# Differential attention: the second exponential ahead of the copy of the transposes, a bank for the second transposes, and the values behind all transposes

## The chip, the cores and the metric

The kernel runs on one core of a Trainium2 chip. A time is device microseconds (us) of one execution of the program; lower is better. PE is TensorE, DVE is VectorE, ACT is ScalarE, POOL is GpSimd and SP is the queue that issues most DMAs. PEld is the loading of weights into TensorE, which overlaps the matmuls of PE.

## The reference

One decoder block over 1024 tokens of width 1024: a state-space mixer and differential attention side by side, merged by gates, then a gated feed-forward network. The change lies in the attention. There are 8 heads; each has two softmaxes, whose difference weighs the values:

```python
for i in range(seq // Q_BLOCK):                  # Q_BLOCK = 128: 8 blocks of queries
    q0, q1 = i * Q_BLOCK, (i + 1) * Q_BLOCK
    s = jnp.einsum('bhqd,bhkd->bhqk', q[:, :, q0:q1], k[:, :, :q1]).astype(f32) * scale
    mask = jnp.arange(q1)[None, :] <= jnp.arange(q0, q1)[:, None]
    p = jax.nn.softmax(jnp.where(mask, s, -jnp.inf), axis=-1)
    p = p.reshape(bsz, DA_HEADS, 2, Q_BLOCK, q1)
    attn = (p[:, :, 0] - lam * p[:, :, 1]).astype(v.dtype)
    outs.append(jnp.einsum('bhqk,bhkd->bhqd', attn, v[:, :, :q1]))
...
gate_ssd, gate_att = jnp.split(jax.nn.sigmoid(gates), N_BRANCH, axis=-1)
merged = gate_ssd * (y_ssd @ w_ssd_o[layer]) + gate_att * (y_att @ w_attn_o[layer])
```

## The kernel before

The attention stage goes through 64 items (j, i): 8 heads j, and in each the 8 blocks i of 128 queries. Block i has (i+1)*128 keys. The order on PE, DVE, ACT and POOL is the order in which the code is written; only SP's is left to a scheduler.

- `scores` computes on PE the products of queries and keys of the two softmaxes, s = 0 and s = 1, into tile `sc`, which lies in one of two pairs of PSUM banks (`ps_mm`). For i below 4 both fit into one pair and one call makes them. For i of 4 and more ("long" blocks) each s has a pair of its own. The pairs alternate, so the scores of (t+2, s=1) get the pair of (t+1, s=1) and start when its exponential has read it.
- `maxima` masks and takes the row maxima on DVE (line 1646 for long blocks), `exps` the exponentials with their sums on ACT (1658 for long blocks, 1655 for short ones). `probs` scales and subtracts the two softmaxes on DVE (1666 to 1668); the result is tile `p`.
- `transposes` turns up to four blocks of `p` on PE (1676) into tile `at`, and ACT copies them to `aT` (1677). A long block has eight at most, so two calls, k0 = 0 and k0 = 4; `at` always lies in the one bank `wb`, and the second call's transposes wait for the copy of the first. `values` multiplies `aT` with the values (1687) one item later. In a head's item t the code writes: scores (t+1, s=1), then scores (t+2, s=0), first transposes of t, maxima and exponential of (t+1, s=1), values of t-1, second transposes of t, maxima (t+2, 0), probs (t+1), exponential (t+2, 0).
- Between the scores `fill` puts the second mixer's gate products (`dense_stream`, tile `gap`): 16 halves of 8 steps, three matmuls of 128x512 a step, one or two steps an item. A half ends with a `tanh` on ACT (1578), which frees its bank. The halves rotate over the two banks `wa` together with tile `ot`.
- `out_o` turns four finished blocks (`ot`, 1712), and ACT copies them out (1719; in the last head 1715 and 1716), after `norm_o` has copied the outputs (`osb`, 1694) and POOL has normed them (1695, 1705).
- After the last item a loop of `NLAST` = 20 rounds, n = 0 to 19, does the last 20 gate steps, one a round. Beside them `att_split` splits the attention's outputs, which DMAs bring back from DRAM into `stg`, into high parts on ACT (line 96, tile `oT`) and low parts on DVE. In round 11 the last `out_o` stands ahead of the step. Then follows the attention's output product, tile `ao`.

Of the kernel before, what the change touches and what calls it, by code (L numbers as in the profile page):

```python
# [11 lines left out]
F32 = mybir.dt.float32  # L12
# [5 lines left out]
P = 128  # L18
D = 1024
S = 1024  # L20
HALF = 512
KD = D // P
# [42 lines left out]
def kernel(ctx: ExitStack, tc: tile.TileContext, a: dict, out: bass.AP, dbg=None):  # L65
# [6 lines left out]
    pp = ctx.enter_context(tc.tile_pool(name="pp", bufs=1, space=bass.MemoryType.PSUM))  # L72
# [10 lines left out]
    def ps_mm(name):  # L83
        return pmm.tile([P, 2, HALF], F32, tag="mm", name=name, bufs=2)

    def ps_wa(name):
        return pp.tile([P, HALF], F32, tag="wa", name=name, bufs=2)

    def ps_wb(name):
        return pp.tile([P, HALF], F32, tag="wb", name=name, bufs=1)  # L90
# [177 lines left out]
    with tc.manual_schedule(engines={EN.PE, EN.DVE, EN.Activation, EN.SP}):  # L268
# [96 lines left out]
        for k in range(2, KD):  # L365
            scale_t(k, 0)
            scale_t(k, 1)
            lows = []
# [245 lines left out]
    f = lambda t: t.rearrange("p c h -> p (c h)")  # L614
# [52 lines left out]
    with tc.manual_schedule(engines={EN.PE, EN.DVE, EN.Activation, EN.SP}):  # L667
# [112 lines left out]
        for m, (kind, *_) in enumerate(pairs):  # L780
# [6 lines left out]
            for p in range(7):  # L787
# [64 lines left out]
                if m == 1 and p == 0:  # L852
                    sm1 = SL.get("sm1", F32, (P, 8, 8, NH))
                    sm2 = SL.get("sm2", F32, (P, 1024))
                    dt, la, acum, _, cd, dte, sp0_ = (sm1[:, n] for n in range(1, 8))
# [23 lines left out]
        m = len(pairs) - 1  # L879
# [305 lines left out]
    def fill(n):  # L1185
        for _ in range(n):
            next(stream, None)
# [215 lines left out]
    with tc.manual_schedule(engines={EN.PE, EN.DVE, EN.Activation, EN.SP}):  # L1403
        split_seq(0)
        old = None
        for n in range(4):
            if n == 0:
                fetch_seq(2)
            ps = ps_mm(f"{seq[n][0]}p{seq[n][1]}")
# [53 lines left out]
        for j in range(8):  # L1463
# [7 lines left out]
            ps = so_half(j, 0)  # L1471
# [54 lines left out]
    blocks = list(range(8))  # L1526
# [26 lines left out]
    highs, lows = deque(), deque()  # L1553
# [5 lines left out]
    def dense_stream():  # L1559
        splits[0], raws[1] = seq_w[12], seq_w[13]  # L1560
        for j in blocks:
            fetch(j + 2)
            while highs:
                one(highs)
            while lows:
                one(lows)
            split_later(j + 1)
            w = splits.pop(j)
            for half in range(2):
                ps = ps_wa(f"gap{j}_{half}")  # L1570
                for k in range(KD):
                    xh_, xl_ = hT[k][half][:, 0, :], hT[k][half][:, 1, :]
                    T.matmul(ps, w[0][:, k, :], xh_, start=(k == 0), stop=False)
                    T.matmul(ps, w[0][:, k, :], xl_, start=False, stop=False)
                    T.matmul(ps, w[1][:, k, :], xh_, start=False, stop=(k == KD - 1))
                    if k < KD - 1:
                        yield
                A.activation(gev[:, half, :], ps, AF.Tanh, scale=0.5)
                SP.dma_start(gad[j][:, half * HALF : (half + 1) * HALF], gev[:, half, :])
                yield  # L1580
# [8 lines left out]
            SP.dma_start(vt[b][:, kt, :], vd[kt][:, j * P : (j + 1) * P])  # L1589

    stream = dense_stream()

    def fill(n):
        for _ in range(n):
            next(stream, None)

    items = [(j, i) for j in range(8) for i in range(8)]

# [49 lines left out]
    def exps(t, s):  # L1648
        if t >= len(items):
            return  # L1650
        i = items[t][1]
        L, bq, sc = (i + 1) * P, i % 2, sc_of.pop((t, s))
        if i < 4:
            for s in range(2):
                A.activation(pt_(t, s)[:, :L], sc[:, s, :L], AF.Exp, bias=nmx[bq][0][:, s : s + 1], accum_out=ssum[bq][:, s : s + 1])
            return
        p = pt_(t, s)[:, :L]
        A.activation(p.rearrange("p (h t) -> p h t", h=2) if i == 4 else p, sc, AF.Exp, scale=-1.0, bias=nmx[bq][s][:, 0:1], accum_out=ssum[bq][:, s : s + 1])  # L1658
# [11 lines left out]
    def transposes(t, k0):  # L1670
        j, i = items[t]
        nk = min(4, i + 1 - k0)
        ptr = ps_wb(f"at{j}_{i}_{k0}")
        at = aTs[t % 2][:, k0 // 4]
        for k in range(nk):
            T.transpose(ptr[:, k * P : (k + 1) * P], pt_(t, 0)[:, (k0 + k) * P : (k0 + k + 1) * P], ident)  # L1676
        A.copy(at[:, :nk].rearrange("p k q -> p (k q)"), ptr[:, : nk * P])  # L1677
# [29 lines left out]
        return [first, second]  # L1707

    def out_o(j, grp):
        ptr = ps_wa(f"ot{j}_{grp}")  # L1710
        for qi in range(4):
            T.transpose(ptr[:, qi * P : (qi + 1) * P], ob[:, qi, :], ident)
        if j == KD - 1:
            o = oT[j][grp] = new_hl(f"oT{j}_{grp}")
            A.activation(oe, ptr, AF.Copy, scale=subw)
            A.activation(o[:, 0, :], oe, AF.Copy)
            V.tensor_tensor(o[:, 1, :], oe, o[:, 0, :].bitcast(F32), op=ALU.subtract)
            return
        A.activation(oe, ptr, AF.Copy, scale=subw)
        SP.dma_start(atd[j][:, grp * HALF : (grp + 1) * HALF], oe)  # L1720
# [3 lines left out]
    parts = [(k, half) for half in range(2) for k in range(KD - 1)]  # L1724
    n_att, n_in = 0, 0
# [31 lines left out]
    NFIRST, NLAST = 6, 20  # L1757
# [4 lines left out]
    with tc.manual_schedule(engines={EN.PE, EN.DVE, EN.Activation, EN.Pool}):  # L1762
# [10 lines left out]
        for t, (j, i) in enumerate(items):  # L1773
            quota = (j * sum(share) + sum(share[: i + 1])) * nfill // (8 * sum(share)) - done
            done += quota
            f1 = (quota + 1) // 2
            if long_(t + 1):
                scores(t + 1, 1)
            fill(f1)
            scores(t + 2, 0)  # L1780
            fill(quota - f1)
            transposes(t, 0)
            if long_(t + 1):
                maxima(t + 1, 1)
                exps(t + 1, 1)
            if t > 0:
                values(t - 1)
            if i >= 4:
                transposes(t, 4)
            maxima(t + 2, 0)  # L1790
            if i % 4 in (1, 2) and norm:
                norm.pop(0)()
            else:
                one(lows)
            probs(t + 1)
            exps(t + 2, 0)
            if i % 4 == 3 and pend is not None:
                out_o(*pend)
                pend = None
            if i % 4 == 0 and t > 0:  # L1800
                jj, ii = items[t - 1]
                pend = jj, ii // 4
                norm = norm_o(*pend)
            else:
                one(highs)
            if t == 56:
                SL.put(*qst[0], *kst[0], *klo[0], vt[0])
                stg = [SL.get(f"stg{i}", F32, (P, 2, HALF)) for i in range(2)]
                for _ in range(4):
                    att_in()  # L1810
            if j < 7 and i == 1:
                load_heads(j + 1)
# [5 lines left out]
        for n in range(NLAST):  # L1818
            if n == 4:
                SP.dma_start(srow2, crowd.broadcast_to([P, D]))  # L1820
            elif n > 4 and n % 2 == 0 and n < 16:
                ada_load()
            if 14 < n < 18:
                ada_sum(False, True)
            if n in (4, 7):
                norm.pop(0)()
            if n == 11:
                out_o(*pend)
            if n == 1:
                fetch_ao(0)  # L1830
            fill(1)
            if n < len(parts):
                att_split()
            if n == 13:
                split_ao(0)
        assert n_att == len(parts) and not highs and not lows
        SL.put(osb, gev, mstrip, *stg)
        for k in range(KD):
            SL.put(*hT[k])
# [39 lines left out]
        for j in range(KD):  # L1879
            w = w_ao.pop(j)  # L1880
            ps = ps_mm(f"ao{j}")
# [768 lines left out]
```

## Time and profile before

| | |
|---|---|
| median of three runs | 1825.58 us (1823.63 to 1826.5) |
| the profiled execution | 1825.24 us |
| its span, first to last instruction | 1823.5 us |
| PE busy in the span | 1770.0 us (97%) |
| DVE busy | 1345.5 us (74%) |
| ACT busy | 916.5 us (50%) |
| the attention's items, by the timeline | about 699.8 to 983.4 us of the span |
| the 20 rounds after them | 983.4 to 1004.8 us |

The profile's times are microseconds from the start of the span. A row of the timeline gives the start, the duration, the engine, the line, the operation, its tiles, and in square brackets how long the engine had stood idle before it and what it waited for. A row of the waits gives who waited for whom, the sum, how often, and the longest. The row of a PE matmul has a modelled end, 0.39 us after its start for 128x512, though the next one starts 0.23 us after it; the idle time of PE is therefore shorter in the profile than the delay of the next matmul, and that of PEld is nearer to it.

### The profile page before, as it was taken

Reading aid. Unit: us, or ns where it says so; the run is one execution under the profiler, and the core shown is the slowest. Engines: PE = TensorE matmul, PEld = TensorE weight load, DVE = VectorE, ACT = ScalarE, POOL = GpSimd, SP = SyncE. Lnnn points to the kernel's source line nnn. Section 1 sums busy time; section 2 is a strip of 40 time slices with the busy share of each in tenths; the row PEclk is TensorE's granted clock in tenths of the full one; section 3 lists DMA queues with packets and bytes.
Section 4 is the critical chain, followed back from the end, with each engine's and each line's share of the span. In section 5 each row is a group of like instructions: output and inputs, shape, how many; then the busy total and the mean of one; then the engine's idle time right before and its main releaser. Section 6 shows DMA issues by size and latency. Waiting matters only on the chain.

```text
span 1823.5 us, 23829 instructions
## 1 busy us (share of the span) xinstructions
PE 1770.0 (97%) x8563; PEld 1459.8 (80%) x8563; DVE 1345.5 (74%) x2048; ACT 916.5 (50%) x1642; POOL 175.8 (10%) x183
## 2 busy tenths in 40 slices
PE   7999999999999999999998999999999999999998
PEld 5788888888778887777776888888888888888887
DVE  7887568854767787777776876678998888876545
ACT  7554345456765213556655132655454454564532
POOL 0000000002551200121111003100000000000001
PEclk9999999999999999999999999999999999999999
DMA  9465653375667798654644979313332223378754
GB/s 375 185 202 169 179 144 99 116 255 166 226 208 236 172 377 231 193 154 129 174 132 141 334 250 378 138 64 110 104 130 107 88 100 118 112 237 305 249 155 157
DMA packets 148330, 337.29 MB, mean 185 GB/s; under 512 B 15570, under 2 KB 50290, under 8 KB 148212
## 3 DMA queue, kind: packets, MB, share of 16 engines
q1 hardware_dynamic: 145012, 325.28, 54.6%
q0 software_dynamic: 3200, 10.49, 1.5%
q8 instruction: 67, 1.10, 0.3%
q14 instruction: 51, 0.42, 0.1%
HBM read 240.46 MB, written 95.25 MB: 184 GB/s over the span
## 4 chain that ended last, share of the span: by engine, by line
PE 56%; DVE 6%; ACT 4%; DMA 3%; issue 2%; SPq 1%; POOL 1%; DVEq 0%; ACTq 0%; POOLq 0%
PE upx L2015 4%; PE upx L2014 4%; PE upx L2016 4%; PE upy L2015 2%; PE upy L2014 2%; PE upy L2016 2%; PE o L1687 2%; PE sc L1612 2%; PE dx L2410 2%; PE dx L2411 2%; PE dx L2409 2%; PE dy L2410 2%; PE dy L2409 2%; PE dy L2411 2%; PE mix L2088 2%
## 5 line engine op out<-in xcount | busy, mean ns | idle before, releaser
L2014 PE MATMUL upx<-t,wu_t 128*128 128x512 f32 x264 | 103.2, 391 | 0.5 <-DVE cv L2474 0.4
L2015 PE MATMUL upx<-t,wu_t 128*128 128x512 f32 x264 | 102.9, 390 | 0.2 <-DVE t L2145 0.2
L2016 PE MATMUL upx<-t,wu_t 128*128 128x512 f32 x264 | 102.8, 389 | 0.0
L1988 ACT ACTIVATE wu_t<-sab 128x512 fp32r<-128x512 f32 x57 | 34.1, 627 | 127.9 <-DVE sab L2005 127.9
L1677 ACT COPY aT<-at 128x512 f32<-128x512 f32 (+2 forms) x96 | 46.0, 479 | 96.4 <-PE at L1676 96.4
L97 DVE TENSOR_TENSOR g_lo<-gst,g_hi 128x1024 fp32r<-128x1024 f32 (+1 forms) x42 | 47.5, 1134 | 50.7 <-ACT g_hi L96 50.6
L1612 PE MATMUL sc<-kst,qst 128*128 128x512 f32 (+3 forms) x192 | 67.2, 355 | 11.4 <-ACT p L1658 11.4
L96 ACT ACTIVATE g_hi<-gst 128x1024 fp32r<-128x1024 f32 (+1 forms) x42 | 41.6, 989 | 67.0 <-DMA gst<-gld_s 36.6
L1687 PE MATMUL o<-vt,aT 128*128 128x128 f32 x576 | 74.8, 275 | 0.0
L1687 PEld LDWEIGHTS o<-vt,aT 128*128 128x128 f32 x576 | 69.3, 192 | 0.6
L1646 DVE CUSTOM_DVE_ANT_0 sc<-sc,mstrip 128x640 f32<-128x640 f32 (+3 forms) x64 | 65.4, 1032 | 5.5 <-PE sc L1613 5.5
L2533 POOL TENSOR_TENSOR rsf<-rsf,nhalf 128x1 f32<-128x1 f32 x8 | 5.2, 655 | 624.3 <-DVE rsf L2532 624.3
L1613 PE MATMUL sc<-klo,qst 128*128 128x512 f32 (+3 forms) x192 | 63.7, 341 | 0.0
L1676 PE MATMUL at<-ident,p 128*128 128x128 f32 x288 | 48.1, 276 | 14.5 <-DVE p L1668 14.4
L1658 ACT ACTIVATE p<-sc,nmx 128x640 f32<-128x640 f32 (+3 forms) x64 | 61.6, 964 | 0.0
L541 PE MATMUL xx<-xt,xw_t 128*128 128x512 f32 x156 | 61.0, 391 | 0.5 <-DVE xcv L830 0.5
L2032 DVE SCALAR_TENSOR_TENSOR ug<-cg,vec,ug 128x1023 f32<-128x1023 f32 (+1 forms) x44 | 56.3, 1279 | 6.1 <-ACT ug L2031 5.3
L543 PE MATMUL xx<-xt,xw_t 128*128 128x512 f32 x156 | 60.7, 389 | 0.0
L542 PE MATMUL xx<-xt,xw_t 128*128 128x512 f32 x156 | 60.7, 389 | 0.0
L2014 PEld LDWEIGHTS upx<-t,wu_t 128*128 128x128 f32 x264 | 49.6, 188 | 11.7 <-DVE cv L2474 1.3
L1992 DVE TENSOR_TENSOR wu_t<-sab,wu_t 128x512 fp32r<-128x512 f32 x57 | 39.3, 689 | 26.5 <-ACT wu_t L1988 26.5
L2015 PEld LDWEIGHTS upx<-t,wu_t 128*128 128x128 f32 x264 | 49.6, 188 | 10.6 <-DVE t L2145 0.5
(579 smaller groups left out, 5725.1 us busy)
## 6 DMA issues: line engine op xcount, KB each, us to landing
adas<-in_w_ada SPq DMA_DIRECT2D x32, 512.0 KB
wuf<-in_w_up SPq DMA_DIRECT2D x22, 512.0 KB
gld_s<-gsum SPq DMA_DIRECT2D x22, 512.0 KB
gst<-gld_s SPq DMA_DIRECT2D x20, 512.0 KB
wdt_raw<-wtd SPq DMA_DIRECT2D x20, 512.0 KB
wuv<-in_w_up SPq DMA_DIRECT2D x19, 512.0 KB
gld_a<-ug SPq DMA_DIRECT2D x33, 256.0 KB
adat<-in_w_ada SPq DMA_DIRECT2D x16, 512.0 KB
```

Source lines behind the costliest of these rows:

```text
L541: T.matmul(o, wh, xh_, start=(k == 0 and first), stop=False, skip_group_check=not first)
L1612: T.matmul(sc, qs_[s][:, tsl], ks_[s][:, n0:n1], start=True, stop=False)
L1613: T.matmul(sc, qs_[s][:, tsl], kl[s][:, n0:n1], start=False, stop=True)
L1646: V.tensor_tensor_reduce(out=sc, in0=sc, in1=strip, scale=-1.0, scalar=BIG, op0=ALU.add, op1=ALU.min, accum_out=nmx[bq][s][:, 0:1])
L1658: A.activation(p.rearrange("p (h t) -> p h t", h=2) if i == 4 else p, sc, AF.Exp, scale=-1.0, bias=nmx[bq][s][:, 0:1], accum_out=ssum[bq][ ...
L1687: T.matmul(po_of[j, grp][:, qi, :], aTs[t % 2][:, kt // 4, kt % 4, :], vt[j % 2][:, kt, :], start=(kt == 0), stop=(kt == i))
L2014: T.matmul(out_, wh, xh_, start=(k == 0 and first), stop=False, skip_group_check=not first)
L2015: T.matmul(out_, wh, xl_, start=False, stop=False, skip_group_check=not first)
L2016: T.matmul(out_, wl, xh_, start=False, stop=(k == end), skip_group_check=not first)
L2409: T.matmul(o, gh[:, kk, tsl], wh, start=(k == 0 and not more), stop=False, skip_group_check=more)
L2410: T.matmul(o, gh[:, kk, tsl], wl, start=False, stop=False, skip_group_check=more)
L2411: T.matmul(o, gl[:, kk, tsl], wh, start=False, stop=(k == KF - 1), skip_group_check=more)
```

## The change

Four edits, all in the attention stage. In an item the maxima and the exponential of (t+1, s=1) are written ahead of the first transposes; the second transposes follow the first, and the values come after both; the second transposes, and `ot`, get bank `wa1`, and all gate halves bank `wa0`, one after the other, where they rotated over the two. A `fill` that would step over the end of a half stops there and owes the rest to the next call. The last `out_o` moves from round 11 to round 14.

```diff
-    def ps_wa(name):
-        return pp.tile([P, HALF], F32, tag="wa", name=name, bufs=2)
+    n_wa = 0
+
+    def ps_wa(name, i=None):
+        nonlocal n_wa
+        if i is None:
+            i, n_wa = n_wa % 2, n_wa + 1
+        return pp.tile([P, HALF], F32, tag=f"wa{i}", name=name, bufs=1)
...
-                ps = ps_wa(f"gap{j}_{half}")
+                ps = ps_wa(f"gap{j}_{half}", 0)
...
     def fill(n):
-        for _ in range(n):
+        nonlocal owed, n_step
+        n, owed = n + owed, 0
+        for m in range(n):
+            if m and n_step % KD == 0:
+                owed = n - m
+                return
             next(stream, None)
+            n_step += 1
...
-        ptr = ps_wb(f"at{j}_{i}_{k0}")
+        ptr = ps_wa(f"at{j}_{i}_{k0}", 1) if k0 else ps_wb(f"at{j}_{i}_{k0}")
...
-        ptr = ps_wa(f"ot{j}_{grp}")
+        ptr = ps_wa(f"ot{j}_{grp}", 1)
...
             fill(quota - f1)
-            transposes(t, 0)
             if long_(t + 1):
                 maxima(t + 1, 1)
                 exps(t + 1, 1)
+            transposes(t, 0)
+            if i >= 4:
+                transposes(t, 4)
             if t > 0:
                 values(t - 1)
-            if i >= 4:
-                transposes(t, 4)
             maxima(t + 2, 0)
...
-            if n == 11:
+            if n == 14:
                 out_o(*pend)
...
             fill(1)
+            if n == NLAST - 1:
+                fill(0)
```

What the engines then get is shown at two places, with the names numbered: `sc4_5_1` is head 4, block 5, s = 1, and `at4_4_0` head 4, block 4, k0 = 0; `p1` holds s = 1. The line numbers of the changed kernel are some ten higher.

ACT in head 4, from the first transposes of block 4 on, before and then changed:

```order
L1677 COPY aT0_5702<-at4_4_0_7171 128x512
L1658 ACTIVATE p1_1_5701,ssum1_5710<-sc4_5_1_7150,nmx1_1_5714 128x768
L1677 COPY aT0_5702<-at4_4_4_7183 128x128
L1658 ACTIVATE p0_2_5699,ssum0_5709<-sc4_6_0_7163,nmx0_0_5711 128x896
L1694 COPY osb_5704<-o4_0_7052 128x512
L1677 COPY aT1_5703<-at4_5_0_7206 128x512
L1658 ACTIVATE p1_0_5700,ssum0_5709<-sc4_6_1_7193,nmx0_1_5712 128x896
L1677 COPY aT1_5703<-at4_5_4_7220 128x256
```

```order
L1670 ACTIVATE p1_1_5701,ssum1_5710<-sc4_5_1_7150,nmx1_1_5714 128x768
L1689 COPY aT0_5702<-at4_4_0_7173 128x512
L1689 COPY aT0_5702<-at4_4_4_7179 128x128
L1670 ACTIVATE p0_2_5699,ssum0_5709<-sc4_6_0_7163,nmx0_0_5711 128x896
L1706 COPY osb_5704<-o4_0_7052 128x512
L1670 ACTIVATE p1_0_5700,ssum0_5709<-sc4_6_1_7193,nmx0_1_5712 128x896
L1689 COPY aT1_5703<-at4_5_0_7208 128x512
L1689 COPY aT1_5703<-at4_5_4_7214 128x256
```

The exponential of s = 1 now stands ahead of both copies; nothing else on ACT moves there.

PE at the same place, before and then changed:

```order
L1575 MATMUL gap4_0_7159<-hT1_0_80,ga4_lo_6775 128x512
L1676 MATMUL at4_4_0_7171<-ident_72,p0_0_5697 128x128 x4
L1687 MATMUL o4_0_7052<-vt0_5689,aT1_5703 128x128 x4
L1676 MATMUL at4_4_4_7183<-ident_72,p0_0_5697 128x128
L1612 MATMUL sc4_6_1_7193<-kst0_1_5510,qst0_1_5508 128x512
L1613 MATMUL sc4_6_1_7193<-klo0_1_5584,qst0_1_5508 128x512
```

```order
L1580 MATMUL gap4_0_7159<-hT1_0_80,ga4_lo_6775 128x512
L1688 MATMUL at4_4_0_7173<-ident_72,p0_0_5697 128x128 x4
L1688 MATMUL at4_4_4_7179<-ident_72,p0_0_5697 128x128
L1699 MATMUL o4_0_7052<-vt0_5689,aT1_5703 128x128 x4
L1624 MATMUL sc4_6_1_7193<-kst0_1_5510,qst0_1_5508 128x512
L1625 MATMUL sc4_6_1_7193<-klo0_1_5584,qst0_1_5508 128x512
```

The values have moved behind the second transposes; what follows is the same.

PE in the rounds after the items, around the end of the half `gap7_0` (round 11), before and then changed; `b12` is a part of the gates' input:

```order
L1575 MATMUL gap7_0_8281<-hT6_0_263,ga7_lo_7954 128x512
L1712 MATMUL ot7_1_8335<-ident_72,osb_5704 128x128 x4
L1573 MATMUL gap7_0_8281<-hT7_0_265,ga7_hi_7953 128x512
L1574 MATMUL gap7_0_8281<-hT7_0_265,ga7_hi_7953 128x512
L1575 MATMUL gap7_0_8281<-hT7_0_265,ga7_lo_7954 128x512
L1573 MATMUL gap7_1_8353<-b12_0_3168,ga7_hi_7953 128x512
```

```order
L1580 MATMUL gap7_0_8281<-hT7_0_265,ga7_lo_7954 128x512
L1578 MATMUL gap7_1_8344<-b12_0_3168,ga7_hi_7953 128x512
L1579 MATMUL gap7_1_8344<-b12_0_3168,ga7_hi_7953 128x512
L1580 MATMUL gap7_1_8344<-b12_0_3168,ga7_lo_7954 128x512
L1578 MATMUL gap7_1_8344<-b12_1_3170,ga7_hi_7953 128x512
L1579 MATMUL gap7_1_8344<-b12_1_3170,ga7_hi_7953 128x512
L1580 MATMUL gap7_1_8344<-b12_1_3170,ga7_lo_7954 128x512
L1724 MATMUL ot7_1_8362<-ident_72,osb_5704 128x128 x4
```

The transposes `ot7_1` now come two steps after the end of the half, and `gap7_1` is in the bank of `gap7_0`.

ACT there, before and then changed:

```order
L96 ACTIVATE oT3_1_8332<-stg1_7980 128x512
L1715 ACTIVATE osb_5704<-ot7_1_8335,subw_3458 128x512
L1716 ACTIVATE oT7_1_8340<-osb_5704 128x512
L1578 ACTIVATE gev_5705<-gap7_0_8281 128x512
L96 ACTIVATE oT4_1_8349<-stg1_7980 128x512
```

```order
L101 ACTIVATE oT3_1_8332<-stg1_7980 128x512
L1583 ACTIVATE gev_5705<-gap7_0_8281 128x512
L101 ACTIVATE oT4_1_8340<-stg1_7980 128x512
L101 ACTIVATE oT5_1_8348<-stg0_7979 128x512
L101 ACTIVATE oT6_1_8354<-stg0_7979 128x512
L101 ACTIVATE wao0_hi_8357<-wao0_raw_8250 128x1024
L1727 ACTIVATE osb_5704<-ot7_1_8362,subw_3458 128x512
L1728 ACTIVATE oT7_1_8367<-osb_5704 128x512
```

The tanh of `gap7_0` stands behind the same eleven splits (rounds 0 to 10) in both; the last copies out of PSUM have moved behind the remaining splits and behind the first split of the output product's weights, `wao0`.

More of the change, by code (lines that the diff above doesn't have):

```diff
@@ L1591 @@
     stream = dense_stream()
+    owed = n_step = 0
     def fill(n):
-        for _ in range(n):
+        nonlocal owed, n_step
[4 more added lines that the diff above has]
+                return
             next(stream, None)
+            n_step += 1
     items = [(j, i) for j in range(8) for i in range(8)]
@@ L1835 @@
                 split_ao(0)
-        assert n_att == len(parts) and not highs and not lows
+        assert n_att == len(parts) and not highs and not lows and n_step == 2 * KD * len(blocks)
         SL.put(osb, gev, mstrip, *stg)
```

## The prediction

> **What bounds the kernel now.** I read the page first, then the stage by windows, then the stage's waits, then the timeline of one head.
>
> ```profile
> span 1823.5 us, 23829 instructions
> PE 1770.0 (97%) x8563; PEld 1459.8 (80%) x8563; DVE 1345.5 (74%) x2048; ACT 916.5 (50%) x1642; POOL 175.8 (10%) x183
> ...
> 699.80:983.40 283.60, 256.90 (x1634) 222.91 (x1634) 210.44 (x478) 169.68 (x410) 46.32 (x45) 1.00 0.54 154
> 856.90:873.55 16.65, 14.71 (x91) 12.71 (x92) 13.45 (x30) 11.37 (x26) 3.09 (x3) 1.00 0.52 144
> ```
>
> The two lower rows are windows: bounds, length, then PE, PEld, DVE, ACT and POOL busy. PE is the bound, and in the attention's items it still stands idle 26.7 of 283.6 us; that is the most any reordering can take. The second row is the long-block half of head 4, where PE idles 1.9 us and DVE is busy 13.45 of 16.65. What PE waits for, from the stage's waits (us in total, times, longest):
>
> ```profile
> PEld sc L1612 <- ACT p L1658: 16.6, 24, 1.0
> PE at L1676 <- DVE p L1668: 14.4, 16, 1.3
> PE sc L1612 <- ACT p L1658: 11.4, 24, 0.8
> PEld gap L1573 <- ACT osb L1719: 1.4, 2, 0.7
> ...
> PE upx L2014 <- DVE cv L2474: 0.4, 1, 0.4
> ```
>
> 24 times, three a head, scores wait for an exponential to free their banks; 16 times, two a head, transposes wait for DVE's result `p`. For the scores, PE's own row counts 11.4 us, the weight loads' 16.6; since a matmul normally starts before the modelled end of the one ahead of it, the larger is the delay, and the smaller its lower bound. The last row is the longest wait of PE behind the attention: what is won there is not waited away later.
>
> **The score waits.** Head 4, from its timeline (start, duration):
>
> ```profile
> 854.99 0.60 ACT L1578 ACTIVATE gev<-gap 128x512 f32<-128x512 f32 x1 [1.80 <-PE gap L1575]
> 856.90 0.19 PEld L1612 LDWEIGHTS sc<-kst,qst 128*128 128x128 f32 x1 [0.65 <-ACT p L1658]
> 859.01 0.14 DVE L1646 DVE_READ_ACCUMULATOR2_ANT nmx<- 128x1 f32 x1
> 860.61 0.59 ACT L1677 COPY aT<-at 128x512 f32<-128x512 f32 x1 [2.30 <-PE at L1676]
> 861.09 0.91 ACT L1658 ACTIVATE p<-sc,nmx 128x768 f32<-128x768 f32 x1
> 861.89 0.20 ACT L1658 ACTIVATION_READ_ACCUMULATOR p<-sc,nmx 128x1 f32 x1
> 862.14 0.19 PEld L1612 LDWEIGHTS sc<-kst,qst 128*128 128x128 f32 x1 [0.75 <-ACT p L1658]
> 864.52 0.14 DVE L1646 DVE_READ_ACCUMULATOR2_ANT nmx<- 128x1 f32 x1
> 865.85 1.01 ACT L1658 ACTIVATE p<-sc,nmx 128x896 f32<-128x896 f32 x1
> 867.01 0.19 PEld L1612 LDWEIGHTS sc<-kst,qst 128*128 128x128 f32 x1 [0.63 <-ACT p L1658]
> ```
>
> The middle wait is the plainest. The maxima of block 5 were ready at 859.15, yet the exponential began at 861.09: ACT stood 2.30 us in front of the copy, which waited for PE's transposes. With the exponential ahead it starts about 1.9 us earlier, and 0.75 suffices. For block 6 the maxima were ready at 864.66 and the exponential began at 865.85: 1.2 earlier, 0.63 suffices. For block 4 the gap is alike (0.65); in this head a tanh (854.99) also stands ahead of it, which leaves a tenth or two. So all 24 waits go, but for that. The copies come later instead, by an exponential at most, and nobody needs them before the values of the next item, some 4 us on.
>
> Not all of it reaches the end of the head, because DVE is next:
>
> ```profile
> 839.38 0.63 PE L1676 MATMUL at<-ident,p 128*128 128x128 f32 x4 [0.97 <-DVE p L1668]
> ...
> 864.45 0.39 PE L1613 MATMUL sc<-klo,qst 128*128 128x512 f32 x1
> 864.99 1.23 DVE L1646 CUSTOM_DVE_ANT_0 sc<-sc,mstrip 128x1024 f32<-128x1024 f32 x1 [0.33 <-PE sc L1613]
> 867.68 1.15 DVE L1668 SCALAR_TENSOR_TENSOR p<-p,coef,p 128x896 f32<-128x896 f32 x1
> 869.13 0.62 PE L1676 MATMUL at<-ident,p 128*128 128x128 f32 x4
> 869.89 0.14 DVE L1646 DVE_READ_ACCUMULATOR2_ANT nmx<- 128x1 f32 x1
> 870.32 1.12 ACT L1658 ACTIVATE p<-sc,nmx 128x1024 f32<-128x1024 f32 x1
> 872.12 1.28 DVE L1668 SCALAR_TENSOR_TENSOR p<-p,coef,p 128x1024 f32<-128x1024 f32 x1
> 873.55 0.63 PE L1676 MATMUL at<-ident,p 128*128 128x128 f32 x4 [0.98 <-DVE p L1668]
> ```
>
> From the last score of block 7, s = 0 (864.45), DVE works without a break through maxima, norm and `probs` to the `p` of block 6 at 868.83; PE's transposes start 0.15 behind such a `p` (873.55 against 872.12 + 1.28), so 4.53 after 864.45. PE comes to them after 4.68, of which 0.63 is the third score wait; without it after 4.05. It then waits some 0.5 there: a new wait. For block 7 the maxima are ready at 870.03 and the exponential began at 870.32, so its `p`, and the wait behind it (873.55), come only some 0.2 earlier. Of the third wait 0.2 comes through. Per head 0.65 + 0.75 + 0.2 = 1.60 of 2.03, so in all 16.6 x 1.60 / 2.03 = **-13.1 us**; by the lower row, 11.4, it is -9.0, and with the third wait in full -16.6.
>
> **The bank for the second transposes, and all transposes ahead of the values.** Before, the values covered the copy that the second transposes waited for. With a bank of their own they need no cover; the copies' ACT time is the same. `ot` shares their bank, behind the values of block 6 (14 matmuls), which cover a copy of 0.59. Cost nothing; without that bank the second transposes would wait for exponential and copy.
>
> **One bank for the gates.** A half's first step now waits for the tanh of the half before. At the start:
>
> ```profile
> 707.97 0.39 PE L1573 MATMUL gap<-b,w_gate_hi 128*128 128x512 f32 x1
> 709.61 0.59 ACT L1578 ACTIVATE gev<-gap 128x512 f32<-128x512 f32 x1
> 712.04 0.52 PE L1676 MATMUL at<-ident,p 128*128 128x128 f32 x3 [0.57 <-DVE p L1668]
> ...
> ACT gev L1578 <- PE gap L1575: 6.9, 9, 1.8
> ```
>
> The second half would start at 710.25 (709.61 + 0.59 and a hand-over of 0.05, as at 862.14) instead of 707.97: 2.3, of which the wait of 0.57 at 712.04 absorbs its part: **+1.7**. At the other boundaries among the items ACT mostly stands ready (the last row: 9 of 16 tanhs found ACT waiting for the gate product), and the next step can start 0.39 + 0.60 + 0.1 = 1.1 after the last matmul's start; four score matmuls between take 0.45 to 0.92 and the step's own 0.23, so a wait is at most 0.4. Four or five boundaries have so little between: **+0.9**. The two waits for `osb` in the list above (1.4) belong to the shared rotation and go: **-1.4**. A `fill` that stops early moves single steps by half an item; on SP some loads of the next head's keys stand one place later, behind a store of `osb`, and they are written six items ahead of their use. Neither costs anything.
>
> **The rounds after the items.**
>
> ```profile
> 986.16 0.60 ACT L1578 ACTIVATE gev<-gap 128x512 f32<-128x512 f32 x1 [0.56 <-PE gap L1575]
> 993.95 1.05 PE L1712 MATMUL ot<-ident,osb 128*128 128x128 f32 x4 [3.06 <-POOL osb L1705]
> 995.21 1.94 ACT L96 ACTIVATE oT<-stg 128x512 fp32r<-128x512 f32 x3 [1.52 <-DMA stg<-atd]
> 997.06 0.67 ACT L1715 ACTIVATE osb<-ot,subw 128x512 f32<-128x512 f32 x1
> 997.78 0.79 PE L1573 MATMUL gap<-b,ga_hi 128*128 128x512 f32 x1 [1.51 <-ACT osb L1715]
> 994.00:996.30 2.30, 2.27 (x7) 1.45 (x7) 0.87 (x2) 1.07 (x2) 0.00 (x0) 0.51 0.86 240
> 997.80:1000.60 2.80, 2.80 (x7) 2.22 (x8) 1.23 (x3) 1.71 (x3) 0.00 (x0) 0.50 0.95 288
> 1000.60:1004.80 4.20, 4.20 (x20) 3.44 (x19) 2.61 (x4) 2.21 (x3) 0.00 (x0) 0.97 0.85 308
> ```
>
> (The last three are windows; the third number from the end is the granted clock.) Round 12 waited for ACT's copy at 997.06, which stood behind splits that wait for DMAs. Now the tanh of round 11 stands in that slot (0.60 for 0.67), and round 12 needs it: PE restarts at 997.7, as before. But it has done less: the transposes have moved behind round 13, and cost 0.5 there. In front of the restart PE runs out of work: round 4 begins at 986.81 behind the tanh, the 24 matmuls of eight steps at some 0.23 end at 992.3, and it idles 5.4 us in one piece instead of 3.06 and 1.51. Before, the clock was half from 994.0 to about 1000.6, and 2.8 us of that lay behind the restart. Now it is half behind the restart for 2.8 us to 6.6; that loses 1.4 to 3.3 us where 1.4 were lost. Middle: 0.5 + 0.9 = **+1.4** (0.5 to 2.4).
>
> [...]
>
> **The sum.** -13.1 + 1.7 + 0.9 - 1.4 + 1.4 = -10.5 us. The profiled execution took 1825.24 us; 1825.24 - 10.5 = **1814.7 us**. The median shown, 1825.58, is 0.34 above that execution, within the spread of the three.
>
> **Rivals.** First: DVE takes over one block earlier, so that the second score wait, too, turns into a wait for `p`. Then 0.65 + 0.2 of 2.03 come through, 7.0 us; with the other terms -4.4, 1820.8 us. For it: DVE is busy 81% in the long blocks. Against it: the exponential that starts 1.9 us earlier lets the `p` of block 5 start earlier as well. Chance 0.11.
>
> Second, the other side: the gates pay at every half's end what they pay at the start. Thirteen halves end among the items; the gain without them is 13.1 + 1.4 - 1.4 = 13.1, so at 1.0 us each nothing is left, from 1.3 the kernel is measurably slower, and at 2.3 it takes 1842 us (1825.24 - 13.1 + 29.9). It decides if ACT reaches the tanh late: exponentials and splits of weights stand ahead of it, as at 709.61. Against it stand the nine tanhs for which ACT was waiting. [...] Chance 0.04.
>
> Third: the exponential gains nothing, since something else than the copy holds it, and the score waits stay. Then 1.7 + 0.9 - 1.4 + 1.4 = +2.6, 1827.8 us, hardly to be told from no change: a measurement of this kernel tells about 0.2% (3.7 us). Against it, the maxima were ready 1.2 to 1.9 us early. Chance 0.05.
>
> **How the numbers follow.** The forecast has 0.78, a third wait won in full (1808 to 1810) 0.02. The forecast's own bounds: best -16.6 + 0.9 - 1.4 + 0.5, start absorbed, 1808.6; worst -9.0 + 2.3 + 2.5 + 2.4, 1823.4. As these do not all fall together, and the first rival belongs in it, the range is 1809 to 1820.8. Faster: 0.78 + 0.02 + most of 0.11 = 0.89; same 0.07; slower 0.04.
>
> **What the profile after would show.** Right: the rows `sc <- ACT p` gone or below 2 us; three waits a head for `p`, the new one of 0.3 to 0.5 at block 6; the starts of block 7's transposes some 1.6 us closer from head to head (873.55 - 839.38 = 34.2 for head 4, so 32.6); a wait of `gap` for the tanh of about 2.3 at the start; PE idle over 5 us near the end of the rounds. Wrong: score waits that stay; a wait for `p` at block 5; many waits of `gap` for `gev`; second transposes that wait for a copy; a half clock for longer than 7 us after the rounds' gap.

## The result and the profile after

| | before | after |
|---|---|---|
| median | 1826.04 us (1823.63 to 1826.79, four runs) | 1814.88 us (1812.19 to 1814.98, four runs) |
| ratio, 95% interval | | 0.9938 (0.992 to 0.9955) |
| profiled execution / span | 1825.24 / 1823.5 us | 1814.90 / 1813.1 us |
| first gate step (start of the items) | 699.84 | 697.92 |
| items, to the end of the last values | 283.51 | 273.16 |
| rounds, to the first matmul of `ao` | 21.43 | 22.27 |
| behind the rounds, to the end of the span | 818.72 | 819.75 |

The kernel is 0.6% faster, against a forecast of 1814.7 us. Of the 10.4 us between the two spans, items and rounds make 10.35 - 0.84 = 9.5. The remaining 0.9 is the difference of two places without an edit: the part ahead of the items was 1.9 us shorter, the part behind the rounds 1.0 longer. In the traces of this study the first gate step stands anywhere from 697.92 to 700.96, so that part of the close hit is luck. Below, I therefore compare items and rounds, not spans.

The page's head after:

```profile
span 1813.1 us, 23867 instructions
...
PE 1766.1 (97%) x8563; PEld 1459.4 (80%) x8563; DVE 1347.0 (74%) x2048; ACT 918.0 (51%) x1642; POOL 175.9 (10%) x183
```

The items as one window (length, then PE, PEld, DVE, ACT and POOL busy; the granted clock is third from the end):

```profile
697.90:971.10 273.20, 253.35 (x1634) 223.14 (x1633) 211.42 (x478) 171.02 (x410) 46.33 (x45) 0.99 0.56 159
```

PE's idle time in the items fell from 26.7 to 19.9 us (273.20 - 253.35). That is less than the 10.35 us won: PE's busy time fell as well, by 3.55, since it covered a part of each score wait (modelled ends, and 0.50 for the first matmul behind a wait where the next has 0.39, as at 856.90 and 857.24 before). The mean clock is 0.99 now; it was 1.00.

The waits in the items after:

```profile
ACT p L1670 <- DVE nmx L1658: 34.2, 26, 2.6
PE at L1688 <- DVE p L1680: 14.2, 20, 1.3
...
PEld gap L1578 <- ACT gev L1583: 4.2, 7, 2.6
PE at L1688 <- ACT ga_hi L1553: 3.3, 3, 1.1
PEld at L1688 <- PE sc L1625: 3.2, 7, 0.5
...
PEld sc L1624 <- ACT p L1670: 0.2, 1, 0.2
```

The 24 score waits (16.6 us) have become one of 0.2. ACT now waits for DVE's maxima (first row), where it stood in front of a copy before. PE's waits for `p` are 20 and 3: a row put down to `ga_hi` is the same wait under another name, as block 7 in the next fence shows (1.11 us, 0.15 behind DVE's `p`). That is three a head, the third at block 6 (seven times also as a PEld row that names `sc`).

Head 4 after, from the timeline:

```profile
845.42 0.52 PE L1688 MATMUL at<-ident,p 128*128 128x128 f32 x3 [0.85 <-DVE p L1680]
852.86 0.91 ACT L1670 ACTIVATE p<-sc,nmx 128x768 f32<-128x768 f32 x1 [0.45 <-DVE nmx L1658]
854.20 0.75 ACT L1689 COPY aT<-at 128x512 f32<-128x512 f32 x2 [0.35 <-PE at L1688]
861.68 0.95 PE L1688 MATMUL at<-ident,p 128*128 128x128 f32 x7 [0.35 <-DVE p L1680]
864.82 1.28 DVE L1680 SCALAR_TENSOR_TENSOR p<-p,coef,p 128x1024 f32<-128x1024 f32 x1
866.25 1.06 PE L1688 MATMUL at<-ident,p 128*128 128x128 f32 x8 [1.11 <-ACT ga_hi L1553]
```

The exponential of block 5 (852.86) starts when its maxima are ready; the copies (854.20, both in one row) come behind it. The new wait is 0.35 us at block 6; block 2 (0.85) and block 7 (1.11) wait as before.

How much a head costs is read from the values of block 7, the only groups of 16: first and last of the eight, after and then before:

```profile
738.36 1.95 PE L1699 MATMUL o<-vt,aT 128*128 128x128 f32 x16
969.13 1.95 PE L1699 MATMUL o<-vt,aT 128*128 128x128 f32 x16
```

```profile
739.28 1.95 PE L1687 MATMUL o<-vt,aT 128*128 128x128 f32 x16
981.40 1.95 PE L1687 MATMUL o<-vt,aT 128*128 128x128 f32 x16
```

From the first to the last, seven heads took 230.77 us for 242.12: 32.97 a head for 34.59, so 1.62 less. Head 0 (from the first gate step to the start of its values of block 7) took 40.44 for 39.44, so 1.0 more. Why, and what the rounds did, the timeline shows (two rows of the start, two of the rounds):

```profile
707.69 0.59 ACT L1583 ACTIVATE gev<-gap 128x512 f32<-128x512 f32 x1
708.34 0.50 PE L1578 MATMUL gap<-b,w_gate_hi 128*128 128x512 f32 x1 [2.12 <-ACT gev L1583]
984.75 0.58 ACT L1583 ACTIVATE gev<-gap 128x512 f32<-128x512 f32 x1
985.38 0.80 PE L1578 MATMUL gap<-b,ga_hi 128*128 128x512 f32 x1 [5.12 <-ACT gev L1583]
```

And a window behind each wait:

```profile
709.50:712.90 3.40, 3.40 (x13) 2.92 (x12) 1.13 (x2) 2.24 (x6) 0.00 (x0) 0.52 1.02 245
985.40:989.40 4.00, 4.00 (x12) 3.25 (x13) 0.86 (x2) 1.17 (x2) 0.00 (x0) 0.50 0.85 289
```

At the start PE stands 2.12 us for the tanh, and from 1.3 us after it restarts, the granted clock is half for 3.4 us; nothing like that was forecast. In the rounds PE stands 5.12 us, and the clock is half for 4.1 us behind it (until 989.5).

### The profile page after: what moved, and what is told of

Read it like the earlier page. It is cut to its first block, busy times and chain, and to the rows that moved or that the text cites. A ratio compares the mean times of both kernels' runs of the same rounds, so it can differ in the third digit from the quotient of the medians.

```text
span 1813.1 us, 23867 instructions
## 1 busy us (share of the span) xinstructions
PE 1766.1 (97%) x8563; PEld 1459.4 (80%) x8563; DVE 1347.0 (74%) x2048; ACT 918.0 (51%) x1642; POOL 175.9 (10%) x183
## 4 chain that ended last, share of the span: by engine, by line
PE 48%; DVE 11%; DMA 6%; ACT 4%; issue 3%; POOL 1%; SPq 0%; DVEq 0%; POOLq 0%; ACTq 0%
PE upx L2029 4%; PE upx L2028 4%; PE upx L2030 4%; PE o L1699 2%; DMA gst<-gld_s 2%; PE upy L2029 2%; PE upy L2028 2%; PE upy L2030 2%; PE mix L2102 2%; PE mix L2104 2%; PE mix L2103 2%; PE so L123 2%; PE so L125 2%; PE so L124 2%; PE sc L1625 1%
## 5 line engine op out<-in xcount | busy, mean ns | idle before, releaser
L1658 DVE CUSTOM_DVE_ANT_0 sc<-sc,mstrip 128x640 f32<-128x640 f32 (+3 forms) x64 | 65.5, 1032 | 13.5 <-PE sc L1625 13.1
L1688 PE MATMUL at<-ident,p 128*128 128x128 f32 x288 | 42.5, 274 | 17.5 <-DVE p L1680 14.2
L2029 PEld LDWEIGHTS upx<-t,wu_t 128*128 128x128 f32 x264 | 49.6, 188 | 10.5 <-DVE t L2159 0.5
```

The costliest lines, as they stand in the source:

```text
L1658: V.tensor_tensor_reduce(out=sc, in0=sc, in1=strip, scale=-1.0, scalar=BIG, op0=ALU.add, op1=ALU.min, accum_out=nmx[bq][s][:, 0:1])
L2029: T.matmul(out_, wh, xl_, start=False, stop=False, skip_group_check=not first)
```

## The experiments

Theory A: the order on ACT (the exponential ahead of the copies) is the whole gain; the bank and the values' place only keep the second transposes from waiting, and the single gate bank costs something at the start and in the rounds. Theory B, in several forms: bank and order carry a part of it. Each kernel ran four or five times (`values between` eleven times) beside the kernel before. "Head 0", "a head" (the mean of heads 1 to 7) and "rounds" are from each kernel's one trace, in us. How far one trace can be trusted shows where kernels are alike: a head takes 32.97, 32.96 and 32.97 us in three of them (after, rounds in two banks, second bank at the start), but the rounds, alike in seven of them, take 21.41 to 23.71.

| kernel | median | ratio, 95% interval | head 0 | a head | rounds |
|---|---|---|---|---|---|
| before | 1825.3 to 1826.0 | 1 | 39.44 | 34.59 | 21.43 |
| after | 1814.88 | 0.9938 (0.992 to 0.9955) | 40.44 | 32.97 | 22.27 |
| exponential alone | 1814.30 | 0.9934 (0.9922 to 0.9946) | 37.61 | 33.20 | 22.09 |
| all but the exponential | 1833.36 | 1.0039 (1.0026 to 1.0051) | 43.26 | 35.23 | 22.17 |
| without the bank | 1842.95 | 1.0086 (1.0071 to 1.01) | 43.56 | 36.96 | 22.23 |
| values between | 1823.54 | 0.9988 (0.9979 to 0.9997) | 41.58 | 34.10 | 22.37 |
| seven steps first | 1814.22 | 0.9937 (0.9924 to 0.9949) | 38.67 | 33.06 | 23.31 |
| second bank at the start | 1813.67 | 0.9936 (0.9923 to 0.995) | 38.39 | 32.97 | 21.41 |
| rounds in two banks | 1810.22 | 0.9916 (0.9902 to 0.9929) | 38.86 | 32.96 | 15.61 |
| `probs` ahead of the norm | 1812.12 | 0.9924 (0.9911 to 0.9936) | 40.22 | 32.57 | 23.71 |
| seven steps, rounds, `probs` | 1807.80 | 0.9897 (0.9882 to 0.9913) | 38.19 | 32.79 | 15.20 |
| exponential alone, rounds | 1811.38 | 0.9922 (0.9909 to 0.9934) | 37.63 | 33.21 | 14.94 |
| second bank, rounds, `probs` | 1806.32 | 0.9894 (0.988 to 0.9907) | 37.88 | 32.60 | 14.94 |

**The exponential alone.** The kernel before, with one move:

```diff
-            transposes(t, 0)
             if long_(t + 1):
                 maxima(t + 1, 1)
                 exps(t + 1, 1)
+            transposes(t, 0)
```

> The kernel before, with only the maxima and the exponential of (t+1, s=1) written ahead of the first transposes; banks, values between the transposes and the last round stay as before. Theory A (the gain is the order on ACT alone): the 24 score waits for the exponential are gone, the first gate half still has a second bank, no 2.1 us wait at the start and no 5 us gap in the rounds; against that the second transposes, which share a bank with the first, now wait for a copy that stands behind an exponential, covered by the values: up to 1 us in the last blocks of a head. Together 1814 to 1818 us, ratio 0.993 to 0.996. Theory B (the exponential needs the second bank and the new order to be worth anything): second transposes wait as long as the scores waited, 1824 to 1828 us.

1814.30 us: not to be told from the whole change. Theory A, though not all score waits go: 5.0 us of them stay, at 16 places. Its waits in the items:

```profile
PEld at L1676 <- ACT aT L1677: 9.4, 9, 1.1
...
PE at L1676 <- DVE p L1668: 7.1, 9, 0.8
...
PEld sc L1612 <- ACT p L1658: 5.0, 16, 0.4
```

Block 6 of head 6, from the timeline (the exponential of block 7 and the copy on ACT, the second transposes on PE):

```profile
929.02 1.11 ACT L1658 ACTIVATE p<-sc,nmx 128x1024 f32<-128x1024 f32 x1 [2.00 <-DVE nmx L1646]
930.13 0.58 ACT L1677 COPY aT<-at 128x512 f32<-128x512 f32 x1
930.76 0.55 PE L1676 MATMUL at<-ident,p 128*128 128x128 f32 x3 [0.91 <-ACT aT L1677]
```

With one bank for both, the second transposes wait for the copy only where it stands behind an exponential that itself waits for the maxima, once a head, in block 6 (0.9 us on PE's row). Elsewhere the values between cover the copy. Against these 9.4 us and the 5.0 of score waits, the waits for `p` are shorter by 10.4: 9 of 7.1 us in all, where the whole change has 23 of 17.5. A head is 0.23 longer than with the whole change, 1.6 over seven heads, and head 0 is 2.8 shorter. So bank, order and gates together bring 1.6 us and cost 2.8 at the start.

**All but the exponential.** The changed kernel with maxima and exponential of (t+1, s=1) behind both transposes.

> The changed kernel with the exponential of (t+1, s=1) put back behind the transposes; the banks, all transposes ahead of the values and the last transposes in round 14 stay changed. Theory A: the score waits are back (about 16 us by the weight loads), the costs of the single gate bank stay, so 1826 to 1830 us, ratio 1.000 to 1.0025. Theory B (bank and order carry the gain): 1814 to 1818 us.

1833.36 us, above Theory A's band too. The sign is A's; the size was missed by at least 3 us. Its score waits in the items:

```profile
PEld sc L1624 <- ACT p L1670: 22.3, 31, 1.0
```

Head 4, from the timeline (ACT twice, PEld twice):

```profile
865.52 0.75 ACT L1689 COPY aT<-at 128x512 f32<-128x512 f32 x2 [2.29 <-PE at L1688]
866.16 0.92 ACT L1670 ACTIVATE p<-sc,nmx 128x768 f32<-128x768 f32 x1
867.22 0.19 PEld L1624 LDWEIGHTS sc<-kst,qst 128*128 128x128 f32 x1 [0.98 <-ACT p L1670]
877.32 0.19 PEld L1624 LDWEIGHTS sc<-kst,qst 128*128 128x128 f32 x1 [0.29 <-ACT p L1670]
```

With both transposes ahead, the exponential stands behind two copies instead of one. The wait of 0.75 became 0.98, and a fourth (0.29) came ahead of block 7's transposes: 22.3 us instead of 16.6. That makes a head 0.64 longer than before, 4.5 us over seven heads. The rest is mainly head 0, 3.8 us longer than before. Without the exponential, the rest of the change loses 7.6 us; with it, nothing that can be told (1814.88 against 1814.30). The parts do not add.

**Without the bank.** `transposes` takes bank `wb` for both calls, all else as changed.

> The changed kernel with the second transposes back in the bank of the first; everything else as changed. Theory A (the bank is needed for the new order): with no values between, each of the 32 pairs of transposes of a long block waits for the exponential and the copy, 0.9 to 1.9 us of which a part falls on waits that exist anyway: 1830 to 1842 us, ratio 1.002 to 1.009, slower than the kernel before. Theory B (the copy is quick enough and the bank idle luxury): 1815 to 1817 us.

1842.95 us, slower than before, as Theory A has it, a little above the upper bound. Its waits for the copy in the items:

```profile
PEld at L1688 <- ACT aT L1689: 40.1, 32, 2.3
```

Block 6 of head 4, from the timeline, in the same order:

```profile
879.59 1.11 ACT L1670 ACTIVATE p<-sc,nmx 128x1024 f32<-128x1024 f32 x1 [1.51 <-DVE nmx L1658]
880.70 0.58 ACT L1689 COPY aT<-at 128x512 f32<-128x512 f32 x1
881.33 0.55 PE L1688 MATMUL at<-ident,p 128*128 128x128 f32 x3 [1.71 <-ACT aT L1689]
```

All 32 second transposes wait, 1.25 us each by the weight loads. Not all of the loss is the waiting itself: the longest waits, 1.7 to 2.1 us in block 6, were followed by a half clock of 3.4 us in four heads of this trace (from 844.5, 882.0, 919.5 and 994.6; there a 128x512 matmul has 0.63 on its row for 0.39). By an estimate from that length each cost 1.7 us. So the bank is worth 28 us, but only because the values no longer stand in between: the move of the values makes the hole that the bank fills.

**Values between.** The changed kernel with `values(t - 1)` between the two transposes again.

> The changed kernel with the values of t-1 again between the first and the second transposes. Theory A (the values' place costs nothing but at block 7, where the transposes of the finished outputs now wait in the shared bank for the copy of the second transposes): 0.5 to 0.9 us at eight or sixteen places, 1819 to 1824 us, ratio 0.996 to 0.9985. Theory B (with a bank of its own for the second transposes, the place of the values is indifferent): 1814 to 1816 us.

1823.54 us: Theory A, near its upper end. Two of its waits in the items:

```profile
PE ot L1724 <- ACT aT L1689: 6.6, 8, 0.8
PEld sc L1624 <- ACT p L1670: 5.1, 16, 0.4
```

One of the eight, in the timeline:

```profile
943.68 0.63 PE L1724 MATMUL ot<-ident,osb 128*128 128x128 f32 x4 [0.82 <-ACT aT L1689]
```

`ot` shares the bank with the second transposes, and now comes right behind the last of them instead of behind 14 more matmuls: the cover that the prediction named (the values of block 6) is gone, and it costs 0.8 us, once a head. Small score waits return at 16 places, as with the exponential alone.

**Seven steps first, second bank at the start.** Two ways to take the 2.1 us at the start away. The first ends the half earlier:

```diff
-    NFIRST, NLAST = 6, 20
+    NFIRST, NLAST = 7, 20
...
-        fill(4)
+        fill(NFIRST - 2)
```

> The changed kernel with seven gate steps ahead of the items instead of six, so that the first half ends one step earlier and its tanh stands on ACT ahead of the exponentials that it stood behind. Theory A (the start of the items costs the changed kernel 2.8 us: 2.1 us of PE standing for the tanh, and a granted clock of half for 3.4 us right behind, which follows from that standing): the wait is gone or below 0.5 us, the clock stays at full, and the time falls by 2.5 to 3 us, 1811.5 to 1812.5 us. Theory B (the half clock there comes of something else, the gates' loads or the start of the attention): the wait goes, the half clock stays, about 1814 us.

The second leaves the steps where they are:

```diff
-                ps = ps_wa(f"gap{j}_{half}", 0)
+                ps = ps_wa(f"gap{j}_{half}", half if j == 0 else 0)
...
-        ptr = ps_wa(f"at{j}_{i}_{k0}", 1) if k0 else ps_wb(f"at{j}_{i}_{k0}")
+        ptr = ps_wa(f"at{j}_{i}_{k0}", 1) if k0 and (j, i) != (0, 4) else ps_wb(f"at{j}_{i}_{k0}")
```

> The changed kernel with the second gate half at the start in the second bank again, and only the second transposes of the first head's block 4 in the bank of the first ones (one place). This takes the 2.1 us standing at the start away by itself and moves no gate step, as the seven steps did. Theory A (in head 0 the standing costs 1.3 us, and the half clock, where it follows, 1.6 more): head 0 takes 37.6 to 38 us for 40.4, 1812 to 1813 us. Theory B (the steps behind it wait for something else then, as with seven steps first): 1814 to 1815 us.

In both, wait and half clock are gone (a 128x512 matmul has 0.39 to 0.48 on its row from 706 to 714 us; with the second bank the clock reads 1.00 from 704 to 716), and head 0 is 1.8 and 2.05 us shorter, less than A's 2.4 to 3: with seven steps the other heads lose 0.6, and with the second bank one second transpose waits 0.73. In total neither can be told from the changed kernel (0.9937, 0.9936 and 0.9938): 1 to 2 us is less than the intervals resolve, and with seven steps the rounds ate it. The tanh of round 11 and the step that waits for it, with seven steps, from the timeline:

```profile
985.20 0.58 ACT L1583 ACTIVATE gev<-gap 128x512 f32<-128x512 f32 x1
985.84 0.80 PE L1578 MATMUL gap<-b,ga_hi 128*128 128x512 f32 x1 [6.06 <-ACT gev L1583]
```

The items ended 0.5 us earlier than in the changed kernel, this tanh came 0.45 us later. It stands behind splits that wait for DMAs (1.41 and 0.21 us right ahead of this tanh in the changed kernel), so what is won ahead of the rounds need not be kept.

**The rounds in two banks.**

```diff
-                ps = ps_wa(f"gap{j}_{half}", 0)
+                ps = ps_wa(f"gap{j}_{half}", half if j == 7 else 0)
...
-        ptr = ps_wa(f"ot{j}_{grp}", 1)
+        ptr = ps_wb(f"ot{j}_{grp}") if (j, grp) == (7, 1) else ps_wa(f"ot{j}_{grp}", 1)
...
-            if n == 13:
+            if n == 3:
                 split_ao(0)
```

> The changed kernel with the last head's two gate halves in two banks again (the last transposes take the bank of the first transposes), and the first split of the output product's weights in round 3 instead of round 13. Theory A (the 5.1 us of PE standing in round 12, and the half clock of 4 us behind it, are the single gate bank): the rounds take 15 to 18 us for 22.3, 1808 to 1811 us. Theory B (the rounds end with the DMAs that bring the attention's outputs back, whatever PE does before): the standing moves behind the last round, in front of the output product, 1813 to 1815 us.

1810.22 us, and 15.61 us of rounds for 22.27: Theory A. Part of it comes back behind the rounds, and the same trace tells something of the start; from the timeline, the start first:

```profile
709.34 0.50 PE L1578 MATMUL gap<-b,w_gate_hi 128*128 128x512 f32 x1 [2.12 <-ACT gev L1583]
...
1009.04 0.50 PE L123 MATMUL ao<-oT,wao_hi 128*128 128x512 f32 x1 [1.08 <-ACT wao_hi L101]
1010.30 0.50 PE L125 MATMUL ao<-oT,wao_lo 128*128 128x512 f32 x1 [0.53 <-DVE wao_lo L102]
```

The window behind that start:

```profile
709.90:713.90 4.00, 4.00 (x27) 3.59 (x26) 2.70 (x9) 3.00 (x8) 0.00 (x0) 1.00 0.94 239
```

The output product, begun earlier, waits 1.6 us for a split of its weights that it did not wait for before. And at the start, which is as in the changed kernel, PE stands the same 2.12 us, yet the clock stays at 1.00. Head 0 takes 38.86 us here for 40.44: the half clock costs 1.6, and the standing with what goes with it 1.25 (38.86 against 37.61 with the exponential alone).

**`probs` ahead of the norm.** On DVE `probs(t + 1)` is written ahead of the norm or the low-part piece.

> The changed kernel with the scaling and subtraction of the softmaxes (t+1) written ahead of the norm and the low-part pieces on DVE. Theory A (DVE is what bounds the items next: the waits of the transposes for p, 14.2 us over 20 places, and the block 6 waits for the scores, 3.2): the waits at blocks 2 and 6 go, those at block 7 shrink, 1805 to 1809 us. Theory B (the pieces are needed soon themselves, or p at these places waits for the exponential and not for DVE): the waits stay or turn into others, 1813 to 1816 us.

1812.12 us, and 32.57 us a head for 32.97. The waits for `p` at blocks 2 and 6 went, as Theory A has it; the gain is a third of what it put on that, since others came (and the rounds were 1.4 us longer in this execution). The last head even became 1.2 us longer (32.13 for 30.93): its block 7 waits 2.2 us for `p`, twice as long as in the others, and a half clock of 3.4 us follows (963.1 to 966.5; the eight transposes take 1.94 us in it, 1.06 in head 4). Two of its waits in the items:

```profile
PE at L1688 <- DVE sqt L1716: 10.1, 8, 2.2
...
PEld sc L1624 <- ACT p L1670: 8.0, 15, 0.9
```

Block 7 of head 4, from the timeline (DVE twice, PE):

```profile
863.62 1.28 DVE L1680 SCALAR_TENSOR_TENSOR p<-p,coef,p 128x1024 f32<-128x1024 f32 x1
864.82 0.15 DVE L1716 TENSOR_TENSOR sqt<-sqt,rsm 128x4 f32<-128x4 f32 x1
865.05 1.06 PE L1688 MATMUL at<-ident,p 128*128 128x128 f32 x8 [1.13 <-DVE sqt L1716]
```

PE starts 0.15 behind the end of `p` (864.90), as in block 7 of the changed kernel: the releaser's name `sqt` is a neighbour's, and the wait is block 7's for `p`. It stays, and score waits are back at 15 places.

**Together.** Seven steps, rounds and `probs`:

> The three previous edits together on the changed kernel: seven steps first, the last halves in two banks with the early split, the softmaxes ahead of the norm on DVE. If the parts add up: 1797 to 1803 us, ratio 0.984 to 0.9875. If the DMAs bound the rounds and DVE's order gains nothing: about 1811 us.

1807.80 us, 0.9897. On the ratios, the parts measured 0.0001, 0.0022 and 0.0014 below the changed kernel and together 0.0041. Within the intervals they add; the result lies between the two cases of the expectation because it had put the single gains too high.

The exponential alone, with the rounds' edits (and its last transposes in round 14):

> The kernel before, with only the exponential ahead of the transposes, and the rounds as in the earlier experiment on them (the last transposes in the bank of the first ones and in round 14, first split of the output product's weights in round 3). Theory A (the bank for the second transposes and the values' place bring nothing that the exponential alone doesn't bring): the items as with the exponential alone, 272 us, the rounds 15.5, and about 1.5 us given back in front of the output product: 1808 to 1810 us, the same as the changed kernel with those rounds. Theory B (the transposes' own bank is worth something once the rounds no longer wait): 1812 us or more.

1811.38 us for the changed kernel's 1810.22 with the same rounds, with overlapping intervals: between A's band and B's, 1.4 us above the first. The items (272.04) and the rounds (14.94) are as forecast. More came back in front of the output product:

```profile
1010.11 0.50 PE L118 MATMUL ao<-oT,wao_hi 128*128 128x512 f32 x1 [2.66 <-ACT wao_hi L96]
1011.36 0.63 PE L120 MATMUL ao<-oT,wao_lo 128*128 128x512 f32 x1 [0.52 <-DVE wao_lo L97]
```

That is 3.2 us for 1.6, and a half clock of 3.4 us followed (from 1011.6, with 0.63 on a matmul's row for 0.39), which the changed kernel with these rounds did not have. So this run can't show that the bank and the order are worth nothing once the rounds no longer wait; the items say that it is little (272.04 for 271.50).

Second bank at the start, rounds and `probs`, the fastest version found:

> The changed kernel with the start's second bank (as above), the last halves in two banks with the early split, and the softmaxes ahead of the norm on DVE. If the gains add (2.5, 4.7 and 2.8 us on 1814.9): 1804 to 1806 us, ratio 0.988 to 0.9895. If the start gives nothing, 1807 us, as the three edits before gave together.

1806.32 us, 0.9894 (0.988 to 0.9907): 1.1% below the kernel before and some 8 us below the changed one (0.0044 of 1825). Whether it needs the bank was not tried: the exponential alone with the rounds' edits and `probs` first has no run.

## Why the prediction was right, point by point

- **The score waits (-13.1).** Right in mechanism and size. The weight loads' count was the right one: a head became 1.62 us shorter where 1.60 was forecast, and the lower row (11.4) would have given 1.1. (The 1.62 also holds the gates' and `osb`'s terms, below.) The third wait came through in part only, as said, because PE then waits 0.35 us for `p` at block 6. The first rival (a wait for `p` at block 5) did not occur: `p` is waited for at blocks 2, 6 and 7 alone. Nor did the third: the exponential by itself gains 11.4 us.
- **The bank and the values (0).** Right as a pair: without the bank 28 us more. What the prediction left out is that the pair isn't needed. With the values between, the first bank serves both calls at 0.9 us and two small score waits a head, and less wait for `p` pays for most of it: a head is 0.23 longer.
- **The start (+1.7).** The mechanism was right, the size was off. The wait came (2.12 us on PE, 2.6 by the weight loads, for 2.3), and with what goes with it cost some 1.25. The step that failed is a term that was not there: a half clock of 3.4 us behind the wait, 1.6 us. Together 2.8.
- **Other boundaries (+0.9), and `osb` (-1.4).** Apart from the start, gate steps waited 1.6 us at six places among the items (4.2 - 2.6, by the weight loads), 0.27 us on average, where four or five places and 0.9 were forecast; the waits for `osb` are gone. They can't be priced apart, but a head came out within 0.05 of the sum's (-11.2 + 0.9 - 1.4 over seven heads, 1.67 each). The second rival, gates that pay at every half's end, is refuted by those 1.6 us.
- **The rounds (+1.4).** Measured +0.84: a gap of 5.12 us for 5.4, and a half clock of 4.1 us behind it, inside 2.8 to 6.6 but below its middle. How near +0.84 comes to +1.4 is partly luck: seven traces with the changed rounds took 21.41 to 23.71, on average 22.50, and the two with the old ones 21.43 and 22.09, so the size is known to about 1 us only.
- **The sum.** Items and rounds were to give -10.5 and gave -9.5. The half clock at the start took 1.6 that no term had, and the other heads fell short by 0.35 (seven times 1.62 for 1.67); the start's wait (1.25 for 1.7) and the rounds (0.84 for 1.4) came out cheaper by 0.45 and 0.55. The two unedited places gave 0.9 back in this execution, and the total came out within 0.2 us of the forecast by that, which is luck. That nothing is waited away behind the attention held for this change (no wait of `ao` for its weights came), but not for the shorter rounds: 1.6 and 3.2 us came back in front of the output product.

## What to carry to other kernels

Where an engine takes its work in the order written (here ACT stood 2.30 us in front of a copy while the maxima of the exponential behind it were ready), look at what stands ahead of the instruction that frees a PSUM bank: here one line moved ahead of a copy was the whole gain, and a bank and a new order were needed only by each other (the moved output was not tried by itself). Test a bundle's parts one by one, both alone and left out: the two answers differ (-11.4 alone; 18.5 lost when left out). When a wait of the bound engine goes, name the next engine's wait in the same block first: here it took 0.4 of the 2.03 us a head.

## What the runs showed of the hardware

The same 2.12 us of standing at the start is in six traces. In five a half clock followed: the changed kernel and the kernels without the exponential, without the bank, with the values between, and with `probs` first (0.50 to 0.52 in windows of 3.2 to 3.4 us). It began within 1.3 us of the restart and lasted 3.4 us. In the sixth, the rounds' experiment, the clock read 1.00 there (709.90 to 713.90, above). The kernel before never showed a half clock among its items (1.00 over 699.80 to 983.40), with waits for `p` up to 1.3 us.

Equal waits also differ within one trace. Without the bank, the second transposes of block 6 wait 1.68 to 1.71 us in heads 0 to 6. A half clock followed in heads 3, 4 and 5, and none in heads 0, 1, 2 and 6. Side by side, with the row of a 128x512 matmul behind the wait where a window doesn't tell:

| kernel | PE stood | until | clock behind it |
|---|---|---|---|
| after, start | 2.12 us | 708.34 | 0.52 (709.50 to 712.90) |
| rounds in two banks, start | 2.12 us | 709.34 | 1.00 (709.90 to 713.90) |
| without the bank, head 4 | 1.71 us | 881.33 | half: 0.63 us on the row at 884.44 |
| without the bank, head 6 | 1.69 us | 957.32 | full: 0.39 us on the row at 959.28 |

So in these traces a standing of about 2 us cost 1.6 us more or did not (head 0: 40.44 against 38.86), and one execution's profile tells only what that execution drew. What decides between the two was not shown.
